# A fourth key block selected by bisection, thirteen steps earlier; one gate in the indexer; two passes on other engines

## The chip, the core and the metric

The kernel runs on one core of a Trainium2 chip. The metric is the device time of one execution in microseconds (us). The median of three runs of the kernel before is 1662.06 us (1661.48 to 1665.17).

The engines are named as the profile names them: PE (matrix products), PEld (the loads of PE's weights), DVE (vector), ACT (scalar functions), POOL (GpSimd) and SP (here it only issues DMAs). Each engine works through its own queue in order.

## The reference

One decoder layer on 1024 tokens of width 1024 in float32. An input projection feeds two attention branches of 8 heads each; the second one attends only to the 256 keys that an indexer scores highest for the query. The branches are gated, merged and projected, and a SwiGLU block follows.

```python
proj = x @ w_in[l]
(fq, fk, fv, f_logit, dq, dk, dv, iq, ik, iw, g_a, g_b) = _split_columns(proj)
...
rel = relu(einsum('bqhd,bkd->bqhk', iqb, ik))              # indexer
score = einsum('bqh,bqhk->bqk', iwb * IDX_SCALE, rel)
score = where(kpos <= qpos, score, NEG_INF)
_, idx = lax.top_k(score, topk)                             # topk = 256
...
merged = sigmoid(g_a) * (o_a @ w_branch_a[l]) + sigmoid(g_b) * (o_b @ w_branch_b[l])
x = layer_norm(ALPHA * x + merged @ w_out[l])
gate, up = split(x @ w_ffn_in[l], 2)
x = layer_norm(ALPHA * x + (silu(gate) * up) @ w_ffn_out[l])
```

## The kernel before

Every float32 product is made of three passes (`mm3`, L96): each operand is split into a rounded high part, which ACT writes, and the rest, a low part that DVE or POOL subtracts (`load_w`, L86, for the weights of the projections: high part on ACT, low part on POOL).

The program has these stages.

- **Indexer** (L242 to L285). Four pieces `c` of the indexer's query weights, two heads each. For each head and each block `i` of 128 queries from 2 to 7, PE makes the scores S (L270, L271), ACT applies relu into one of three tiles `r` (L273, L275), and DVE adds them into the score tile `SM[i]` (L277, L279). `SM[i]` has 128 rows of queries and 128(i+1) keys. Here the order on every engine, PE too, is set by the scheduler that builds the program.
- **Attention** (L540 to L602), 64 steps: eight units of a head pair, two heads, four groups G of two query blocks in the order 3, 0, 2, 1. PE's order is written out by hand: in step k the scores of step k+1 (`weigh`), the transposes and sums of step k (`average`), and between them single groups of three matmuls from a list of filler work: the projections of the next unit and the 16 gates, `NG` of them in each unit. The other engines' order is the scheduler's, which follows the order of the program text where two instructions are both ready. A step's path runs S on PE (L463, L466), maximum on DVE (L473), exp on ACT (L474), reciprocal on DVE (L480), scaling on POOL (L483), transposes on PE (L506), high part on ACT (L507), low part on DVE (L508), sums on PE (L515, L516).
- **Selection of 256 keys** for blocks 2 to 7, needed when the second branch begins at step 32. It is written into the program at step `KSEL` = 31, and the scheduler fills gaps of DVE and ACT with it from the end of the indexer on. Blocks 2, 3 and 4 go by `select_by_max` (L287): 32 times a DVE instruction that finds eight maxima (L290) and one that strikes them out (L291). Blocks 7, 6 and 5 go by `select_by_bisection` (L294): 32 rounds, each of which counts on ACT how many scores of each block are above a threshold (L310, one instruction a block) and then sets the next threshold with three small DVE instructions (L311, L320, L318). At its end DVE makes the masks in pieces of 512 keys (L348 to L361); L361 is the last pass, which turns 1 and 0 into 0 and a large negative number.
- **Branch products, output product, first layer norm** (L605 to L772), not touched.
- **SwiGLU** by a scheme of fewer products (L775 to L904). For each of 22 chunks, DVE makes four sums of weights (`ss`, L843 to L846), and `split` (L793) makes the parts: high on ACT, low on POOL (L795).
- **Output of SwiGLU** (L909 to L1014), not touched.

Of the kernel before, what the change touches and what calls it, by code (L numbers as in the profile page):

```python
# [8 lines left out]
F32 = mybir.dt.float32  # L9
# [11 lines left out]
KT = 8  # L21
# [10 lines left out]
LAG = 2  # L32
W = (1, 1, 1, 1)
PW = 512
BIS = ((7, 6, 5),)
IDX_SCALE = (8 ** -0.5) * (64 ** -0.5)

NMM, NT = 2, 2
AHEAD, LASTC, HURRY = 3, 8, 100
NG = (1, 1, 2, 2, 2, 2, 2, 4)  # L40
ORDER = (3, 0, 2, 1)
PHB, PLB = 3, 3
A1 = (1, 2, 2, 2)
VD, LEAD, KSEL = 4, 5, 31

C_FQ, C_FK, C_FV, C_DQ, C_DK, C_DV, C_IQ, C_GA, C_GB, C_MISC = 0, 4, 8, 12, 16, 20, 24, 28, 36, 44

# [2 lines left out]
def trunk_kernel(ctx: ExitStack, tc: tile.TileContext, xT, xn, wt, wbr, wout, wfi, wfo,  # L50
# [187 lines left out]
    sp.dma_start(ald.rearrange("h r t -> (h r) t"), f(arr[0:16]))  # L238
    sp.dma_start(alkd, f(arr[32:34]))


    for c in range(4):  # L242
        w = split_w(raw0, pool) if c == 0 else load_w(wt[C_IQ + c])
        iq = [idx.tile([128, 768], F32R, name="iq", tag="iq", bufs=4) for _ in range(2)]
        for q, (half, c0, n, d0) in enumerate(((0, 256, 256, 0), (1, 0, 512, 256))):
            ps = ps_mm()
            proj_half(ps[:, :n], w, half, c0=c0, n=n)
            for a in range(2):
                src = ps[a * 64:a * 64 + 64, :n]
                t = iq[a][:, d0:d0 + n]  # L250
                act.activation(t[0:64], src, AF.Copy)
                dve.tensor_tensor(t[64:128], src, f(t[0:64]), op=OP.subtract)
        for a in range(2):
            h = 2 * c + a
            for i in range(2, 8):
                n = 128 * (i + 1)
                nch = 1 if n <= 512 else 2
                m = n // nch
                if nch == 1 and i == 2:
                    S = [psA.tile([128, 512], F32, name="S", tag="O", bufs=1)]  # L260
                elif i == IDXT:
                    S = [psA.tile([128, 512], F32, name="S", tag="T", bufs=NT) for _ in range(2)]
                else:
                    S = [ps_s(nch)]
                lq = iq[a][:, (i - 2) * 128:(i - 1) * 128]
                r = idx.tile([128, L], F32, name="r", tag="r", bufs=3)
                rv = r[:, :n].rearrange("p (a b) -> p a b", a=nch)
                for x in range(nch):
                    o = S[x][:, :m] if len(S) == nch == 2 else (S[0][:, x, :m] if nch == 2 or i == 3 else S[0][:, :m])
                    te.matmul(o, lq, ik1[:, x * m:x * m + m], start=True, stop=False)  # L270
                    te.matmul(o, lq, ik2[:, x * m:x * m + m], start=False, stop=True)  # L271
                    if len(S) == nch:
                        act.activation(rv[:, x], o, AF.Relu, scale=wab[:, i - 2, h:h + 1])  # L273
                if len(S) < nch:
                    act.activation(rv, S[0][:, :, :m], AF.Relu, scale=wab[:, i - 2, h:h + 1])  # L275
                if h == 0:
                    dve.tensor_scalar(SM[i], r[:, :n], sgn[:, i - 2, h:h + 1], None, op0=OP.mult)  # L277
                else:
                    dve.scalar_tensor_tensor(SM[i], r[:, :n], sgn[:, i - 2, h:h + 1], SM[i],  # L279
                                             op0=OP.mult, op1=OP.add)  # L280
    for i in range(2, 8):
        dg = SM[i][:, i * 128:]
        pool.affine_select(dg, dg, pattern=[[-1, 128]], base=0, channel_multiplier=1,
# [10 lines left out]
    def select_by_bisection(blocks, tag):  # L294
# [50 lines left out]
        for x, i in enumerate(blocks):  # L345
# [4 lines left out]
            for c in range(0, 128 * (i + 1), 512):  # L350
# [7 lines left out]
                if c + m < 128 * (i + 1):  # L358
                    dve.tensor_tensor(ci, ci, cum[:, m - 1:m], op=OP.subtract)
                dve.scalar_tensor_tensor(Sc, Sc, ki, e, op0=OP.is_gt, op1=OP.add)  # L360
                dve.tensor_scalar(Sc, Sc, BIG, BIG, op0=OP.mult, op1=OP.subtract)  # L361


    at, _at = open_pool("at")

    def proj_steps(ps, w, half):

        hi, lo = w
        for k in range(KT):
            mm3(ps, [(hi[:, k * 128:k * 128 + 128], lo[:, k * 128:k * 128 + 128],  # L370
                      XH[half][:, k], XL[half][:, k])], k == 0, k == KT - 1)
            yield

    def gate(br, c):
        w = load_w(wt[(C_GA, C_GB)[br] + c])
        for h in range(2):
            ps = ps_mm()
            yield from proj_steps(ps, w, h)
            g = at.tile([128, 512], F32, name="g", tag="g", bufs=2)
            if (br, c) == (1, 7):  # L380
                with tc.high_priority(offset=HURRY):
                    act.activation(g, ps, AF.Tanh, scale=0.5)
            else:
                act.activation(g, ps, AF.Tanh, scale=0.5)
            sp.dma_start(gdr[br][c, :, h * 512:h * 512 + 512], g)

    def project(br, pr, made):
        qc, kc, vc = ((C_FQ, C_FK, C_FV), (C_DQ, C_DK, C_DV))[br]
# [144 lines left out]
            sp.dma_start(odr[br][hd // 2, r0:r0 + 64, G * 256:G * 256 + 256], o)  # L533
            yield

    gates = [gate(br, c) for br in range(2) for c in range(8)]
    units = [[] for _ in range(8)]
    late = []

# [37 lines left out]
    for k, (n, a, G) in enumerate(todo):  # L577
# [4 lines left out]
        slots = [back] * nb  # L582
        slots.insert(A1[G], ahead)
        slots.insert(0, ahead)
        if k == KSEL:
            for blocks in BIS:
                select_by_bisection(blocks, blocks[0])
            for i in range(2, 8):
                if not any(i in blocks for blocks in BIS):
                    select_by_max(i)  # L590
# [199 lines left out]
        ring.append(at_)  # L790
        return at_[0].tile([128, 2, 512], F32R, name="w", tag=at_[1], bufs=at_[2])

    def split(s, raw):  # L793
        act.activation(s[:, 0], raw, AF.Copy)  # L794
        pool.tensor_tensor(s[:, 1], raw, f(s[:, 0]), op=OP.subtract)  # L795

    def product(ps, w, x, first=True, last=True):
        mm3(ps, [(w[:, 0, k * 128:k * 128 + 128], w[:, 1, k * 128:k * 128 + 128], x[0][:, k], x[1][:, k])
# [35 lines left out]
    for c in range(FC):  # L834
# [12 lines left out]
        if new:  # L847
            split(a11, g1_)
            split(a12, g2_)
        split(s2, r2)  # L850
        split(s3, r3)
        split(s1, r1)
        split(s4, r4)
# [214 lines left out]
```

## Time and profile before

| | |
|---|---|
| median of three runs | 1662.06 us |
| the profiled execution | 1662.34 us |
| its span, first to last instruction | 1660.5 us |
| busy in the span: PE, DVE, ACT, POOL | 96%, 69%, 47%, 45% |

The span is what the profile covers; 1.8 us of the execution lie around it. A busy share is an average over stages with different limits. A matmul is drawn longer than the time for which it holds PE, so PE's idle time shows only part of what a wait costs; the number of matmuls in a stretch shows the rest.

### The profile page before, as it was taken

How to read it: one execution, taken by the hardware profiler on the slowest of the kernel's cores; microseconds unless marked ns; L12 is line 12 of the kernel's file. 1: busy time of each engine (PE TensorE's matmuls, PEld its weight loads, DVE VectorE, ACT ScalarE, POOL GpSimd, SP SyncE). 2: the span in 40 equal slices, each digit the busy share in tenths (PEclk: the TensorE clock that was granted, in tenths of full speed). 3: DMA queues.
4: the chain of work that ended last, by engine and by line, in shares of the span. 5: the costliest groups of instructions: out<-in, count | busy, mean ns of one | idle time of the engine just before them, and what ended most of it. 6: DMA issues, size and time to landing. Idle time of an engine off the chain costs nothing. (4 is left out here: it accounts for less than half of the span.)

```text
span 1660.5 us, 22523 instructions
## 1 busy us (share of the span) xinstructions
PE 1601.0 (96%) x7722; PEld 1309.5 (79%) x7722; DVE 1139.2 (69%) x1986; ACT 772.6 (47%) x1374; POOL 749.9 (45%) x748
## 2 busy tenths in 40 slices
PE   7899999999999999999899998999999999999997
PEld 5777887777788888888778877778888888878886
DVE  6889999988744444444585665666666666757686
ACT  6777887885444545455442024223222322354341
POOL 1122333332323333334452044766777676487673
PEclk9999999999999999999999998999999999999999
DMA  5112212121212121212776112554445444598652
GB/s 179 47 40 66 61 46 60 51 72 46 61 53 77 52 77 52 77 52 76 260 248 226 58 59 93 194 172 149 155 154 168 152 146 134 180 328 307 194 163 100
DMA packets 96379, 202.83 MB, mean 122 GB/s; under 512 B 10820, under 2 KB 37444, under 8 KB 96264
## 3 DMA queue, kind: packets, MB, share of 16 engines
q1 hardware_dynamic: 96264, 201.39, 37.4%
q8 instruction: 61, 1.00, 0.3%
q14 instruction: 54, 0.44, 0.1%
HBM read 139.40 MB, written 53.03 MB: 116 GB/s over the span
## 5 line engine op out<-in xcount | busy, mean ns | idle before, releaser
L99 PE MATMUL mm<-xh,whi 128*128 128x512 f32 (+1 forms) x720 | 296.9, 412 | 14.1 <-ACT whi L147 6.5
L101 PE MATMUL mm<-xl,whi 128*128 128x512 f32 (+1 forms) x720 | 282.1, 392 | 1.0 <-DVE xl L157 0.9
L100 PE MATMUL mm<-xh,wlo 128*128 128x512 f32 (+1 forms) x720 | 281.4, 391 | 0.5 <-DVE wlo L148 0.5
L483 POOL TENSOR_SCALAR p<-p,st 128x512 f32<-128x512 f32 (+1 forms) x192 | 113.8, 602 | 318.7 <-DVE st L480 266.0
L93 POOL TENSOR_TENSOR wlo<-wraw,whi 128x1024 fp32r<-128x1024 f32 x43 | 103.4, 2406 | 164.2 <-ACT whi L92 164.1
L101 PEld LDWEIGHTS mm<-xl,whi 128*128 128x128 f32 x720 | 136.2, 189 | 32.2 <-DVE xl L157 2.2
L99 PEld LDWEIGHTS mm<-xh,whi 128*128 128x128 f32 x720 | 137.3, 191 | 28.6 <-ACT whi L147 6.5
L795 POOL TENSOR_TENSOR w<-ss,w 128x512 fp32r<-128x512 f32 x88 | 121.9, 1404 | 73.4 <-ACT w L794 73.4
L100 PEld LDWEIGHTS mm<-xh,wlo 128*128 128x128 f32 x720 | 137.5, 191 | 13.0 <-DVE wlo L148 1.0
L508 DVE TENSOR_TENSOR pl<-T,ph 128x512 fp32r<-128x512 f32 (+1 forms) x160 | 100.6, 634 | 36.6 <-ACT ph L507 33.7
L100 PE MATMUL acc<-fs 128*128 128x512 f32 x308 | 120.1, 390 | 1.3 <-DVE fs L935 1.3
L101 PE MATMUL acc<-fs 128*128 128x512 f32 x308 | 119.9, 389 | 0.6 <-POOL fs L936 0.6
L99 PE MATMUL acc<-fs 128*128 128x512 f32 x308 | 119.8, 389 | 0.0
L507 ACT ACTIVATE ph<-T 128x512 fp32r<-128x512 f32 (+1 forms) x160 | 87.3, 552 | 40.7 <-PE T L506 38.2
L310 ACT ACTIVATE junk<-sm,nt 128x1024 bf16<-128x1024 f32 (+2 forms) x93 | 96.8, 1040 | 14.5 <-DVE nt L318 12.6
L506 PE MATMUL T<-identf,p 128*128 128x128 f32 x576 | 91.0, 274 | 5.0 <-POOL p L483 2.9
L936 POOL TENSOR_TENSOR fs<-fraw,fs 128x512 fp32r<-128x512 f32 x47 | 80.8, 1733 | 27.1 <-ACT fs L934 27.1
L506 PEld LDWEIGHTS T<-identf,p 128*128 128x128 f32 x576 | 71.6, 140 | 27.0 <-POOL p L483 4.6
L812 ACT ACTIVATE u<-u 128x512 f32<-128x512 f32 x22 | 13.9, 632 | 168.2 <-DVE u L811 168.2
L843 DVE TENSOR_TENSOR ss<-wup 128x512 f32<-128x512 f32 x22 | 34.4, 1565 | 83.4 <-POOL w L795 71.5
L516 PE MATMUL O<-pl,V 128*128 128x256 f32 x320 | 82.9, 282 | 1.8 <-DVE pl L508 1.8
L515 PE MATMUL O<-ph,V 128*128 128x256 f32 x320 | 83.9, 284 | 0.0
(285 smaller groups left out, 4259.3 us busy)
## 6 DMA issues: line engine op xcount, KB each, us to landing
wraw<-in_wt_dram SPq DMA_DIRECT2D x45, 512.0 KB
fraw<-abd SPq DMA_DIRECT2D x30, 512.0 KB
wraw<-in_wfi_dram SPq DMA_DIRECT2D x25, 512.0 KB
wup<-in_wfi_dram SPq DMA_DIRECT2D x22, 512.0 KB
wb<-in_wfo_dram SPq DMA_DIRECT2D x44, 256.0 KB
abd<-wb SPq DMA_DIRECT2D x88, 128.0 KB
abd<-h SPq DMA_DIRECT2D x44, 256.0 KB
abd<-u SPq DMA_DIRECT2D x33, 256.0 KB
```

What stands on the lines that cost most here:

```text
L93: pool.tensor_tensor(lo, raw, f(hi), op=OP.subtract)
L99: te.matmul(ps, ah, bh, start=(first and i == 0), stop=False)
L100: te.matmul(ps, al, bh, start=False, stop=False)
L101: te.matmul(ps, ah, bl, start=False, stop=(last and i == n - 1))
L310: act.activation(j[:, :128 * (i + 1)], SM[i], AF.Sign, bias=bias(x), accum_out=s[:, x:x + 1])
L483: pool.tensor_scalar(pc, pc, st[:, 3:4], 1.0, op0=OP.mult, op1=OP.mult)
L506: te.transpose(T[:, s * 128:s * 128 + 128], P[qq][:, j * 128:j * 128 + 128], identf)
L507: act.activation(ph[:, c:], T[:, c:], AF.Copy)
L508: dve.tensor_tensor(pl[:, c:], T[:, c:], f(ph[:, c:]), op=OP.subtract)
L515: te.matmul(O, V[:, j, :], ph[:, r0:r0 + 256], start=(j == 0), stop=False)
L516: te.matmul(O, V[:, j, :], pl[:, r0:r0 + 256], start=False, stop=(last and jj == 1))
L795: pool.tensor_tensor(s[:, 1], raw, f(s[:, 0]), op=OP.subtract)
```

## The change

Five edits. (1) `BIS` takes block 4 into the bisection, so each round counts four blocks and `select_by_max` is left with blocks 2 and 3. (2) The bisection is written into the program at step `KBIS` = 18 instead of 31. (3) The masks' last pass (L361 before) is a POOL instruction. (4) Gate 0 leaves the attention's filler and is computed in the indexer, one half in piece 0 and one in piece 1; `NG` falls from 2 to 1 in unit 2, and the gates of units 0 to 2 move up by one, so that unit 2 (steps 16 to 23) has one gate fewer. (5) In the first chunk of SwiGLU the low part of `s2` is subtracted on DVE instead of POOL.

```diff
-BIS = ((7, 6, 5),)
+BIS = ((7, 6, 5, 4),)
-NG = (1, 1, 2, 2, 2, 2, 2, 4)
+NG = (1, 1, 1, 2, 2, 2, 2, 4)
-VD, LEAD, KSEL = 4, 5, 31
+VD, LEAD, KBIS, KSEL = 4, 5, 18, 31
...
+    def half_gate(br, c, w, h, tile):
+        ps = ps_mm()
+        yield from proj_steps(ps, w, h)
+        g = tile()
...
+            act.activation(g, ps, AF.Tanh, scale=0.5)
+        sp.dma_start(gdr[br][c, :, h * 512:h * 512 + 512], g)
...
+        if c == 0:
+            wg = load_w(wt[C_GA])
+        first = half_gate(0, 0, wg, c, lambda: idx.tile([128, L], F32, name="r", tag="r", bufs=3)[:, :512]) \
+            if c < 2 else iter(())
...
+                if a or i > 4:
+                    next(first, None)
+        for _ in first:
+            pass
...
-                dve.tensor_scalar(Sc, Sc, BIG, BIG, op0=OP.mult, op1=OP.subtract)
+                pool.tensor_scalar(Sc, Sc, BIG, BIG, op0=OP.mult, op1=OP.subtract)
...
-    gates = [gate(br, c) for br in range(2) for c in range(8)]
+    gates = [gate(br, c) for br in range(2) for c in range(8)][1:]
...
-        if k == KSEL:
+        if k == KBIS:
             for blocks in BIS:
                 select_by_bisection(blocks, blocks[0])
+        if k == KSEL:
             for i in range(2, 8):
...
-    def split(s, raw):
+    def split(s, raw, eng=pool):
         act.activation(s[:, 0], raw, AF.Copy)
-        pool.tensor_tensor(s[:, 1], raw, f(s[:, 0]), op=OP.subtract)
+        eng.tensor_tensor(s[:, 1], raw, f(s[:, 0]), op=OP.subtract)
...
-        split(s2, r2)
+        split(s2, r2, pool if c else dve)
```

How the queues move is shown at three places. The line numbers of the changed kernel are 11 to 27 higher for the same code; rows of before stand first.

PE in the indexer, from the scores of the first head's block 3 on (`S` are scores, `mm_568` is the projection of piece 1, `mm_502` the gate's first half):

```order
L270 MATMUL S_474<-ik1_275,iq_408 128x512
L271 MATMUL S_474<-ik2_276,iq_408 128x512
L99 MATMUL mm_568<-xh0_78,whi_562 128x256
L100 MATMUL mm_568<-xh0_78,wlo_563 128x256
L101 MATMUL mm_568<-xl0_79,whi_562 128x256
L270 MATMUL S_514<-ik1_275,iq_409 128x384
L271 MATMUL S_514<-ik2_276,iq_409 128x384
L99 MATMUL mm_568<-xh0_78,whi_562 128x256
L100 MATMUL mm_568<-xh0_78,wlo_563 128x256
L270 MATMUL S_480<-ik1_275,iq_408 128x320
```

In the changed kernel, at the same place:

```order
L293 MATMUL S_480<-ik1_275,iq_408 128x512
L294 MATMUL S_480<-ik2_276,iq_408 128x512
L99 MATMUL mm_502<-xh0_78,whi_470 128x512
L100 MATMUL mm_502<-xh0_78,wlo_471 128x512
L101 MATMUL mm_502<-xl0_79,whi_470 128x512
L99 MATMUL mm_502<-xh0_78,whi_470 128x512
L100 MATMUL mm_502<-xh0_78,wlo_471 128x512
L293 MATMUL S_486<-ik1_275,iq_408 128x320
L294 MATMUL S_486<-ik2_276,iq_408 128x320
```

The gate's matmuls take the places between scores that the next piece's projection had, and that projection moves behind them.

ACT in the attention, from the 20th to the 21st step (`junk` is a count of the bisection, `p` an exp, `ph` a high part, `Q1` and `K1` parts of a projection, `o` the end of a step):

```order
L310 ACTIVATE junk_4700,s7_4458<-sm7_196,nt7_4453 128x1024
L310 ACTIVATE junk_4702,s7_4458<-sm6_195,nt7_4453 128x896
L474 ACTIVATE p_3265,st_3266<-S_3259,st_3266 128x1024
L530 ACTIVATE o_3289<-O_3222 64x256
L310 ACTIVATE junk_4704,s7_4458<-sm5_194,nt7_4453 128x768
L507 ACTIVATE ph_3311<-T_3310 128x512
L474 ACTIVATE p_3303,st_3304<-S_3299,st_3304 128x128
L399 ACTIVATE Q1_3160<-mm_3252 64x512
```

In the changed kernel, in the 21st step:

```order
L337 ACTIVATE junk_3449,s7_3154<-sm7_196,nt7_3149 128x1024
L518 ACTIVATE ph_3823<-T_3822 128x512
L337 ACTIVATE junk_3451,s7_3154<-sm6_195,nt7_3149 128x896
L421 ACTIVATE K1_3080<-mm_3742 64x512
L337 ACTIVATE junk_3453,s7_3154<-sm5_194,nt7_3149 128x768
L421 ACTIVATE K1_3084<-mm_3742 64x512
L337 ACTIVATE junk_3455,s7_3154<-sm4_193,nt7_3149 128x640
L485 ACTIVATE p_3843,st_3844<-S_3839,st_3844 128x256
L518 ACTIVATE ph_3850<-T_3849 128x512
```

A round now has four counts, and in steps 19 to 23 almost every second instruction of ACT's queue is one. Counted in the whole queue, steps 12 to 23 hold 45 counts before and 64 now.

DVE at the end of the 25th step, where the masks are made (`junk` and `e`, `cum` are mask passes, `pl` the low part that the step's last sums need):

```order
L473 TENSOR_REDUCE st_3776<-S_3771 128x1
L357 SCALAR_TENSOR_TENSOR e_4780<-cum_4781,s7_4458,e_4780 128x512
L508 TENSOR_TENSOR pl_3786<-T_3784,ph_3785 128x512
L480 RECIPROCAL st_3776<-st_3776 128x1
L359 TENSOR_TENSOR s7_4458<-s7_4458,cum_4781 128x1
L360 SCALAR_TENSOR_TENSOR sm7_196<-sm7_196,k7_4460,e_4780 128x512
L349 TENSOR_SCALAR s7_4458<-s7_4458 128x1
L348 TENSOR_SCALAR junk_4813,s7_4458<-sm5_194,k7_4460 128x768
L361 TENSOR_SCALAR sm7_196<-sm7_196 128x512
L508 TENSOR_TENSOR pl_3805<-T_3803,ph_3804 128x384
```

In the changed kernel, up to the same low part:

```order
L376 TENSOR_SCALAR s7_3154<-s7_3154 128x1
L375 TENSOR_SCALAR junk_3558,s7_3154<-sm6_195,k7_3156 128x896
L383 SCALAR_TENSOR_TENSOR cum_3544<-e_3543 128x512
L376 TENSOR_SCALAR s7_3154<-s7_3154 128x1
L375 TENSOR_SCALAR junk_3576,s7_3154<-sm5_194,k7_3156 128x768
L384 SCALAR_TENSOR_TENSOR e_3543<-cum_3544,s7_3154,e_3543 128x512
L376 TENSOR_SCALAR s7_3154<-s7_3154 128x1
L375 TENSOR_SCALAR junk_3594,s7_3154<-sm4_193,k7_3156 128x640
L386 TENSOR_TENSOR s7_3154<-s7_3154,cum_3544 128x1
L387 SCALAR_TENSOR_TENSOR sm7_196<-sm7_196,k7_3156,e_3543 128x512
L376 TENSOR_SCALAR s7_3154<-s7_3154 128x1
L519 TENSOR_TENSOR pl_4270<-T_4268,ph_4269 128x384
```

Before, five mask instructions stand between that low part and the reciprocal ahead of it; now there are fifteen, of which the last eleven are shown.

## Rows read from the trace of the kernel before

**Rows 1.** The page: PE's line of section 1 and PE's granted clock in 40 slices
```profile
PE 1601.0 (96%) x7722; PEld 1309.5 (79%) x7722; DVE 1139.2 (69%) x1986; ACT 772.6 (47%) x1374; POOL 749.9 (45%) x748
...
PEclk9999999999999999999999998999999999999999
```

**Rows 2.** Windows: stretch, its length, busy us (instructions) of each engine, granted clock, DMA
```profile
core 0: us, PE busy (x) PEld busy (x) DVE busy (x) ACT busy (x) POOL busy (x), PEclk, DMA share, GB/s
32.00:76.00 44.00, 36.75 (x188) 29.89 (x187) 35.57 (x47) 33.65 (x47) 6.06 (x3) 1.00 0.14 34
...
162.00:253.00 91.00, 89.55 (x498) 72.87 (x496) 88.76 (x223) 73.38 (x155) 30.23 (x53) 1.00 0.20 55
253.00:379.00 126.00, 120.73 (x660) 97.56 (x658) 112.12 (x254) 105.28 (x212) 41.70 (x68) 1.00 0.22 62
379.00:410.00 31.00, 27.22 (x136) 21.93 (x135) 27.50 (x67) 14.65 (x31) 7.25 (x12) 0.89 0.10 31
410.00:441.00 31.00, 28.73 (x150) 22.89 (x149) 28.00 (x45) 13.29 (x27) 12.39 (x16) 1.00 0.20 67
441.00:503.00 62.00, 62.00 (x344) 52.00 (x343) 28.62 (x64) 30.57 (x63) 21.66 (x34) 1.00 0.22 59
1016.00:1028.00 12.00, 8.31 (x25) 6.30 (x24) 8.44 (x9) 6.17 (x12) 11.07 (x9) 0.72 0.22 68
```

**Rows 3.** Windows of L310 alone: ACT's busy us (rows, two a count)
```profile
253.00:379.00 126.00, 50.29 (x90) 1.00 0.22 62
```

**Rows 4.** Waits of PE's weight loads, 30 to 110 us: total us, times, longest
```profile
PEld S L270 <- ACT r L275: 9.7, 18, 3.0
```

**Rows 5.** Waits of PE's weight loads, 110 to 441 us
```profile
PEld S L463 <- ACT p L474: 7.4, 10, 1.3
...
PEld T L506 <- DVE pl L508: 4.1, 5, 1.9
```

**Rows 6.** Timeline of PE at 48 us: start, us, what
```profile
48.27 0.39 PE L99 MATMUL mm<-xh,whi 128*128 128x512 f32 x1
48.49 0.40 PE L100 MATMUL mm<-xh,wlo 128*128 128x512 f32 x1
```

**Rows 7.** Groups by shape, DVE, 100 to 440 us: busy us, mean ns | idle before
```profile
L290 DVE MAX8 m<-sm 128x8 f32<-128x640 f32 x32 | 26.1, 817 | 0.1
L291 DVE MATCH_REPLACE8 sm<-m,sm 128x640 f32<-128x640 f32 x32 | 25.8, 808 | 0.0
```

**Rows 8.** Groups by shape, ACT, 100 to 440 us: the bisection's counts
```profile
L310 ACT ACTIVATE junk<-sm,nt 128x1024 bf16<-128x1024 f32 x31 | 35.6, 1147 | 13.8 <-DVE nt L318 12.6 <-DVE mp L329 0.9
L310 ACT ACTIVATE junk<-sm,nt 128x896 bf16<-128x896 f32 x31 | 32.2, 1040 | 0.4
...
L310 ACT ACTIVATE junk<-sm,nt 128x768 bf16<-128x768 f32 x31 | 29.0, 934 | 0.4
...
L310 ACT ACTIVATION_READ_ACCUMULATOR junk<-sm,nt 128x1 f32 x93 | 17.9, 192 | 0.0
```

**Rows 9.** Groups by shape, DVE, 100 to 440 us: passes of the masks
```profile
L356 DVE TENSOR_TENSOR_SCAN cum<-e 128x512 f32<-128x512 bf16 x4 | 6.6, 1645 | 0.0
L360 DVE SCALAR_TENSOR_TENSOR sm<-sm,k,e 128x512 f32<-128x512 f32 x4 | 3.0, 748 | 0.0
...
L348 DVE TENSOR_SCALAR_CACHE_REDUCE junk<-sm,k 128x768 bf16<-128x768 f32 x1 | 1.0, 1001 | 0.0
```

**Rows 10.** Timelines of DVE and POOL at 430 us
```profile
429.77 2.64 DVE L361 TENSOR_SCALAR sm<-sm 128x256 f32<-128x256 f32 x1
...
429.54 2.45 POOL L93 TENSOR_TENSOR wlo<-wraw,whi 128x1024 fp32r<-128x1024 f32 x1
```

**Rows 11.** Timelines of PE, DVE and POOL in SwiGLU's first chunk
```profile
1022.43 0.80 PE L100 MATMUL pb<-t2h,w 128*128 128x512 f32 x1 [3.69 <-POOL w L795]
...
1017.04 1.79 DVE L846 TENSOR_TENSOR ss<-wraw,ss 128x512 f32<-128x512 f32 x1
...
1019.36 0.68 DVE L843 TENSOR_TENSOR ss<-wup 128x512 f32<-128x512 f32 x1
...
1021.12 1.26 POOL L795 TENSOR_TENSOR w<-ss,w 128x512 fp32r<-128x512 f32 x1
```

More of the change, by code (lines that the diff above doesn't have):

```diff
@@ L239, in trunk_kernel, with proj_steps @@
     sp.dma_start(alkd, f(arr[32:34]))
+    def proj_steps(ps, w, half):
+        hi, lo = w
+        for k in range(KT):
+            mm3(ps, [(hi[:, k * 128:k * 128 + 128], lo[:, k * 128:k * 128 + 128],
+                  XH[half][:, k], XL[half][:, k])], k == 0, k == KT - 1)
+            yield
+    def half_gate(br, c, w, h, tile):
+        ps = ps_mm()
+        yield from proj_steps(ps, w, h)
+        g = tile()
+        if (br, c) == (1, 7):
+            with tc.high_priority(offset=HURRY):
+                act.activation(g, ps, AF.Tanh, scale=0.5)
+        else:
+            act.activation(g, ps, AF.Tanh, scale=0.5)
+        sp.dma_start(gdr[br][c, :, h * 512:h * 512 + 512], g)
     for c in range(4):
@@ L360, in select_by_bisection @@
                 dve.scalar_tensor_tensor(Sc, Sc, ki, e, op0=OP.is_gt, op1=OP.add)
-                dve.tensor_scalar(Sc, Sc, BIG, BIG, op0=OP.mult, op1=OP.subtract)
+                pool.tensor_scalar(Sc, Sc, BIG, BIG, op0=OP.mult, op1=OP.subtract)
     at, _at = open_pool("at")
[L366 to L372, printed above, removed]
     def gate(br, c):
@@ L376, in gate @@
         for h in range(2):
[L377 to L385, printed above, removed]
+            yield from half_gate(br, c, w, h, lambda: at.tile([128, 512], F32, name="g", tag="g", bufs=2))
     def project(br, pr, made):
```

## The prediction

> **What bounds the kernel now.** I read the page first. PE is busy for 1601 of 1660.5 us [rows 1], so whatever the change does counts only where PE waits or where PE has less to do. The slices are too coarse to show where that is, so I cut the span into stretches. From 441 to 503 us, when the selection is over, PE is busy in every microsecond and does 344 matmuls in 62.00 us, 0.180 us each [rows 2]. That is the pace of the attention with no other engine in its way, and I measure the earlier stretches by it; their mix of matmuls is nearly the same.
>
> - 162 to 253 us: 498 matmuls would take 89.6 us at that pace, the stretch took 91.
> - 253 to 379 us: 660 would take 118.8, it took 126. DVE is busy for 112.12 and ACT for 105.28 of it [rows 2].
> - 379 to 410 us: 136 would take 24.5, it took 31, at a granted clock of 0.89, so part of it ran at 1.2 instead of 2.4 GHz. DVE is busy for 27.50.
> - 410 to 441 us: 150 would take 27.0, it took 31, with DVE busy for 28.00 [rows 2].
>
> So the selection costs PE some 19 us between 162 and 441 us, and DVE is the busiest of the other engines in all four stretches. The waits agree: PE's weight loads stand for an exp on ACT (7.4 us in ten waits) and for low parts on DVE (4.1 us in five) [rows 5]. In the indexer PE is idle for 7.25 us between 32 and 76 us [rows 2], mostly because a score tile has not been read yet by the relu on ACT (9.7 us in 18 waits of the loads, pieces 2 and 3 included) [rows 4]. In SwiGLU's first chunk there is one wait of 3.69 us for a low part on POOL [rows 11].
>
> **The gate in the indexer.** It takes 48 matmuls of 512 columns out of steps 16 to 23 and puts them into pieces 0 and 1. Two such matmuls start 0.22 to 0.23 us apart [rows 6], so this is 10.9 us of PE on both sides. PE's idle time there is 7.25 us, and the order puts the gate's matmuls between the scores where PE waits. If they fill it, the indexer gets longer by 10.9 - 7.25 = 3.6 us. If they fill none of it, by 10.9; if they also fill what the drawn-out ends of matmuls hide, by nothing. I take **+3.5 us**, near the row of PE's idle time, and keep 0 to +8. What comes along costs nothing: one high part on ACT and one low part on POOL, both with idle time there (33.65 and 6.06 busy of 44) [rows 2], two Tanh on ACT, and two stores on SP. Behind these stores SP's queue has weights that are needed only by the first projections, some 30 us later. A store holds one of the three `r` tiles until it lands; the next piece's projection, which needs no `r`, covers that. Without that cover a store's time would be lost to the relu twice.
>
> **Block 4 by bisection.** DVE loses 32 maxima of 817 ns and 32 strikes of 808 ns [rows 7], 52 us in all, most of it between 253 and 379 us. ACT gets 32 more counts. The counts of 1024, 896 and 768 keys take 1147, 1040 and 934 ns [rows 8], 106 ns less for each 128 keys, so I estimate 828 ns for 640 keys, and 192 ns to read the sum. What matters is where they fall.
>
> - Up to step 11 (162 to 253 us) blocks 2 and 3 are still searched by maxima, so DVE stays as full as it was (88.76 of 91), and each round puts one more count on ACT, which has 73.38 of 91 [rows 2]. Ten rounds add some 9 us there. Nothing is relieved. I take **+1.0 us**, between 0 and +3.
> - Steps 12 to 23 (253 to 379 us). The 45 counts of before are busy for 50.29 us [rows 3], 1.118 us each. With 640 keys in the mix the mean falls by 0.053 us (the mean of 1147, 1040, 934 and 828 is 987, of the first three 1040). The order now holds 64 counts in these steps: 64 x 1.065 = 68.2 us, 17.9 more. The gate takes about 2.2 us away (a high part and two Tanh). ACT's load is 105.3 + 17.9 - 2.2 = 121 us. PE's need falls to 118.8 less seven eighths of 10.9, which is 109. DVE's falls from 112 to about 60. So ACT takes DVE's place as the engine that sets the pace, with 121 us of work for a stretch that took 126. Part of the busy time is the tail of an instruction beside the next one, and ACT's queue has a count or a step's instruction ready nearly always. Against that, a step's exp and high parts now wait for one count more each time. I take 123.5 us, **-2.5 us**. The lower end is PE's need and the 4 us for waits that no edit touches, 115 (-11). The upper end is ACT at 93% of the time, 130 (+4).
>
> **Thirteen steps sooner, and the masks.** The order finishes the bisection in the 23rd step, as before: the earlier place in the program makes up for the longer rounds, it does not bring the masks forward. But the masks now stand ahead of the steps in the program, and the scheduler puts them into DVE's queue in larger blocks. Their work grows by block 4: two count passes (1001 ns at 768 keys, so near 0.9 each), a scan of 1645 ns and a smaller one, and four compare passes of 750 ns or less [rows 9], about 7 us. The last pass, now on POOL, gives back some 4.9 us, 2.64 of it from a single instruction of 256 keys that ran beside a low part of POOL [rows 10]. DVE's load in 379 to 441 us stays near 57 of 62 us. In the 25th step, fifteen mask instructions stand between a reciprocal and the low part that the step's last sums need: 0.9 to 1.3 us for each of four counts, 1.6 for the scan, three passes of 0.5 to 0.75 and seven small ones, about 7 us. PE has about 3.5 us of other work until then (three groups of filler and eight sums), so I expect one wait of about **4 us** there and, as after the waits of before, a few microseconds at 1.2 GHz. Before, this stretch lost 6.5 us in several waits; PE has one eighth of the gate less in it. I set the two stretches to **-1.0 us**, between -4 and +4. POOL's last passes go behind its scaling of the probabilities; with 19.6 of 62 us busy there [rows 2] they cost nothing, and without that slack up to eight times 0.6 us.
>
> **The low part on DVE.** POOL makes the first chunk's `s2` low part as its third and ends it at 1022.4 us, and PE starts then. On DVE it goes behind the sum that is followed by the instruction at 1019.36, so it would end at 1020.0 at 0.68 us, or at 1021.1 at the 1.79 us that a subtraction of the same shape took beside POOL [rows 11]. PE starts 1.3 to 2.4 us sooner, and a shorter wait can save time at the lower clock, which was 0.72 on average here [rows 2]. The next product needs a low part that POOL makes now at about the same time as before, so some of it is lost again. **-1.5 us**, between -4 and +0.5.
>
> The row of 1.79 us fits a rule of the Trainium skill, "SBUF — State Buffer", section "Who interferes with whom": a DVE instruction with two inputs in SBUF and a GpSimd instruction that reads SBUF cannot use the port that they share at the same time, and the second waits. This speaks against the fifth edit and for the third. By the rule alone the low part would end at 1021.1 and the term would be about -1; without it -2.5.
>
> **Sum.** +3.5 + 1.0 - 2.5 - 1.0 - 1.5 = -0.5 us on the profiled execution of 1662.34 us. The median lies 0.28 us lower, so I forecast **1661.6 us**, no change that can be measured. A measurement of this kernel tells about 0.2%, 3.3 us, from no change.
>
> **Rivals.**
>
> *Faster: DVE was the limit, and ACT holds.* For it speaks that DVE is the busiest in all the slow stretches. If ACT's counts fit between the step's own instructions, 253 to 379 us shrink to 115 (-11), and with the other terms the sum is -9: **1653 us**. Against it: ACT's load of 121 us is above PE's 109.
>
> *Slower: ACT's queue becomes the wait.* Place: steps 18 to 23, where every second instruction is a count. Each exp and each high part stands behind a count of about 1 us, and PE, whose score tiles and transpose tiles come free only through them, stands too. Price: with ACT at 93%, the stretch takes 130 us (+4), and the wait at the masks brings +2 in place of -1; with the other terms as taken 3.5 + 1.0 + 4 + 2 - 1.5 = +9: **1671 us**. It decides against the change as soon as ACT can't be kept busy for 97% of the stretch. Against it: before, ACT was idle only 12.6 us for the bisection's own chain [rows 8], and DVE, which answers it, is free now.
>
> *The masks don't come sooner and the gate is only moved.* This is the forecast itself, 1661.6 us: time taken from steps 16 to 23 on PE is given to ACT, and the gate is paid in the indexer.
>
> **How the numbers follow.** Forecast (within 0.2%): 0.38. Faster rival: 0.33, since a wait less for DVE may give more than the loads show. Slower rival: 0.29. The range reaches into both: with the stretch at 115 the sum is -9, 1653, and the fastest tenth beyond that is left out; with the slower rival's sum it is 1671, and what is above that is left out. I give 1653 to 1671. The likeliest case's own range is 1659 to 1665.
>
> **What would show it.** In the changed kernel: the indexer's last score 3 to 4 us later; the end of the 11th step about 4 us later; between there and the 23rd step's end about 123 us, with ACT busy for over 95% and DVE for under 60%; one wait of PE for a low part on DVE of about 4 us in the 25th step; the wait in SwiGLU's first chunk 1 to 2 us shorter. The forecast is wrong if steps 12 to 23 take under 119 or over 128 us, or if the indexer takes as long as before.

## The result, and the profile after

The changed kernel takes 1672.28 us, median of six runs (1669.45 to 1676.23); the kernel before, run beside it, 1661.50 us. The ratio is 1.0069, with a 95% interval of 1.0058 to 1.0080: **slower by 0.7%**, 1.3 us outside of the forecast's range (1653 to 1671), with the sign of the slower rival. The profiled execution took 1670.48 us, which lies inside the range, with a span of 1668.7 us. So the profiles explain 8.2 of the 10.8 us between the medians; the other 2.6 lie between executions, and no profile shows them.

The page of the changed kernel, its span and its busy times [rows 1]:

```profile
span 1668.7 us, 22516 instructions
...
PE 1602.4 (96%) x7722; PEld 1312.3 (79%) x7722; DVE 1095.3 (66%) x1899; ACT 797.5 (48%) x1438; POOL 761.9 (46%) x755
```

PE's busy time has hardly changed, DVE lost 44 us and ACT got 25: the change did to the engines' loads what it says. To see where the time went I compare marks of the work: the end of the sum `o` that closes an attention step (L531 before, L542 now), and in SwiGLU the start of the same matmul, counted from PE's last one. The table shows what each stretch of work added to the lead or the lag of a kernel against the kernel before, each in its profiled execution; the first line is the length of the stretch before. "SwiGLU 0" goes from 1009 to 1066 us of the kernel before; the last stretch is the rest. Steps are counted from 1 here; `KBIS`, `KSEL` and the steps named with them count from 0.

| kernel | to end of step 1 | steps 2-11 | 12-18 | 19-23 | 24-28 | 29-64 | to SwiGLU | SwiGLU 0 | rest | to the last matmul |
|---|---|---|---|---|---|---|---|---|---|---|
| before (us) | 161.9 | 91.1 | 71.6 | 54.3 | 62.2 | 358.3 | 209.4 | 57.5 | 585.3 | |
| changed | +10.3 | +2.0 | -6.4 | +4.3 | +0.8 | -0.4 | +0.3 | -3.4 | +0.9 | +8.5 |
| gate_back | -4.0 | +2.2 | -4.5 | +5.5 | +1.5 | -0.7 | -1.5 | -3.4 | +2.4 | -2.5 |
| gate_only | +9.2 | +0.8 | -6.3 | -5.8 | -2.8 | +2.0 | -1.6 | -0.1 | -0.7 | -5.2 |
| own_tile | +4.7 | +2.0 | -6.4 | +5.5 | +3.0 | -0.4 | -0.9 | -3.4 | +1.2 | +5.4 |
| split_back | +10.3 | +2.0 | -6.4 | +4.3 | +0.7 | -0.4 | +0.6 | -0.0 | -1.8 | +9.3 |
| gate_own | +4.4 | +0.8 | -6.2 | -6.1 | -2.0 | +1.6 | -1.1 | -0.1 | -0.1 | -8.7 |
| bis_back | +10.2 | +0.8 | -6.3 | +2.8 | -6.6 | -0.2 | -0.2 | -3.4 | +1.9 | -1.0 |
| kbis31 | +11.1 | +2.0 | -6.2 | -5.7 | -5.6 | +7.7 | +1.4 | -3.4 | +1.5 | +2.7 |
| gate_own_split | +4.6 | +0.7 | -6.2 | -6.1 | -2.2 | +1.6 | -1.3 | -3.4 | +2.1 | -10.1 |
| mask_back | +9.1 | +2.0 | -6.3 | +4.4 | +1.4 | -1.7 | +0.3 | -3.4 | +1.6 | +7.4 |
| best_mask | +4.5 | +0.7 | -6.2 | -6.1 | -0.9 | -0.3 | +0.4 | -3.4 | +1.6 | -9.7 |
| best_k24 | +3.8 | +0.7 | -6.2 | -6.1 | +2.4 | -0.8 | +0.7 | -3.3 | +2.5 | -6.3 |

So the changed kernel has lost everything when the first step ends, and the rest of it wins 1.8 us back. The last score of the indexer ends at 120.83 us, where it was 109.68: 11.2 us, the gate's 10.9 us of PE in full. The windows of the changed kernel, for the stretches of [rows 2], show it as well (the stretch, its length, busy us and instructions of each engine, granted clock, DMA):

```profile
core 0: us, PE busy (x) PEld busy (x) DVE busy (x) ACT busy (x) POOL busy (x), PEclk, DMA share, GB/s
32.00:76.00 44.00, 36.16 (x165) 28.93 (x164) 30.02 (x41) 30.19 (x41) 5.05 (x2) 0.96 0.15 38
...
172.20:265.40 93.20, 90.03 (x499) 73.02 (x498) 88.97 (x222) 82.20 (x174) 29.83 (x52) 1.00 0.19 54
...
265.40:389.10 123.70, 115.50 (x629) 92.61 (x629) 65.51 (x159) 118.02 (x249) 36.45 (x65) 0.99 0.20 51
389.10:452.10 63.00, 52.38 (x264) 41.76 (x263) 58.00 (x119) 28.15 (x58) 36.12 (x38) 0.95 0.19 56
```

In the first row PE is idle for 7.84 us, where it was 7.25 before: most of the gate is in this stretch (its second half up to the 20th of 24 matmuls), and none of the idle time is gone. In the third row ACT is busy for 118 of 123.7 us and DVE for 65.5, as forecast.

**The indexer.** PE's timeline (start, us, what; in brackets the idle time before it and what ended it), then ACT's:

```profile
49.49 0.40 PE L101 MATMUL mm<-xl,whi 128*128 128x512 f32 x1
...
55.76 0.28 PE L101 MATMUL mm<-xl,whi 128*128 128x256 f32 x1
58.57 0.50 PE L99 MATMUL mm<-xh,whi 128*128 128x512 f32 x1 [2.54 <-ACT r L257]
...
59.46 0.63 PE L99 MATMUL mm<-xh,whi 128*128 128x512 f32 x1
59.89 0.63 PE L100 MATMUL mm<-xh,wlo 128*128 128x512 f32 x1
```

```profile
56.77 1.26 ACT L296 ACTIVATE r<-S,wab 128x512 f32<-128x512 f32 x2
57.92 0.60 ACT L257 ACTIVATE r<-mm 128x512 f32<-128x512 f32 x1
```

The first row is the last matmul of the gate's first half, done at 49.9 us. Its tanh (L257) starts at 57.92 us, 8 us later: it wants one of the three tiles `r`, and these go round between the relus on ACT and the sums on DVE. Until then the half gate holds one of the two accumulators `mm`. The 256 columns of piece 1's projection fill the other one by 56.0 us, and the 512 columns that must follow have none. So PE stands for 2.54 us, and the piece's scores, which stand behind that projection in PE's order, start at 65.75 us. Before, the 512 columns were made between the scores of piece 0, from 43.12 to 55.8 us (two of their matmuls are in [rows 6]), and the scores of piece 1 start at 55.60 us.

**Steps 19 to 23.** ACT's timeline at 338 us (`junk` is a count, `p` an exp, `ph` a high part) and PE's:

```profile
338.64 0.69 ACT L485 ACTIVATE p<-S,st 128x512 f32<-128x512 f32 x1
...
339.32 1.14 ACT L337 ACTIVATE junk<-sm,nt 128x1024 bf16<-128x1024 f32 x1
...
340.45 0.47 ACT L518 ACTIVATE ph<-T 128x384 fp32r<-128x384 f32 x1
```

```profile
340.98 0.38 PE L526 MATMUL O<-ph,V 128*128 128x256 f32 x1 [2.54 <-ACT ph L518]
```

PE stops at 338.44 us and waits for a high part that stands behind an exp and a count of 1024 keys. The same happens at 362.2 us (1.29 us). In all PE waits 7.2 us in these steps: 3.8 for high parts on ACT, 2.4 for POOL's scaling and 1.0 for low parts on DVE.

**Step 25.** The wait that the prediction named is there, and matmuls of 512 columns behind it start 0.43 us apart and not 0.23:

```profile
414.09 0.48 PE L527 MATMUL O<-pl,V 128*128 128x256 f32 x1 [4.51 <-DVE pl L519]
414.80 0.63 PE L99 MATMUL mm<-xh,whi 128*128 128x512 f32 x1
```

**SwiGLU.** The first chunk gains 3.4 us, and a chunk further on loses more. In the first chunk PE waits twice in place of the 3.69 us of before [rows 11], for the low part on DVE and, at the next product, for one on POOL:

```profile
1031.07 0.50 PE L100 MATMUL pb<-t2h,w 128*128 128x512 f32 x1 [1.35 <-DVE w L807]
...
1035.39 0.50 PE L100 MATMUL pb<-t3h,w 128*128 128x512 f32 x1 [1.26 <-POOL w L807]
```

The rest of the gain goes along with the clock. The granted clock of 18 us from the same matmul on was 0.81 and is 1.00 now; the windows of before and of the changed kernel:

```profile
1014.00:1032.00 18.00, 14.31 (x51) 11.09 (x50) 11.32 (x13) 6.98 (x13) 15.07 (x13) 0.81 0.29 91
```

```profile
1024.60:1042.60 18.00, 15.39 (x65) 11.88 (x65) 14.48 (x15) 7.49 (x14) 14.61 (x12) 1.00 0.27 92
```

PE, DVE and POOL at 1080 us:

```profile
1086.79 0.77 PE L99 MATMUL pb<-t3h,w 128*128 128x512 f32 x1 [4.22 <-DVE u L875]
```

```profile
1080.94 1.77 DVE L857 TENSOR_TENSOR ss<-wraw,wup 128x512 f32<-128x512 f32 x1 [4.32 <-POOL w L807]
```

```profile
1071.46 1.29 POOL L807 TENSOR_TENSOR w<-ss,w 128x512 fp32r<-128x512 f32 x1
1076.40 0.82 POOL L894 TENSOR_TENSOR wb<-wb 128x256 f32<-128x256 f32 x1 [3.65 <-DMA wb<-in_wfo_dram]
...
1079.61 2.54 POOL L807 TENSOR_TENSOR w<-ss,w 128x512 fp32r<-128x512 f32 x2
```

The scheduler has put four subtractions of output weights (`wb`) ahead of the low parts (`w`). They wait until 1076.40 us for a DMA; a sum of DVE (L857) waits for the low part behind them, and the sum `u` that PE needs stands behind that one on DVE.

### The profile page after: what moved, and what is told of

Same layout as the page of the kernel before. It is cut to its first block, busy times and chain, and to the rows that moved or that the text cites. A ratio compares the mean times of both kernels' runs of the same rounds, so it can differ in the third digit from the quotient of the medians.

```text
span 1668.7 us, 22516 instructions
## 1 busy us (share of the span) xinstructions
PE 1602.4 (96%) x7722; PEld 1312.3 (79%) x7722; DVE 1095.3 (66%) x1899; ACT 797.5 (48%) x1438; POOL 761.9 (46%) x755
## 4 chain that ended last, share of the span: by engine, by line
PE 71%; DVE 11%; ACT 6%; DMA 4%; POOL 4%; issue 4%; SPq 0%; DVEq 0%; POOLq 0%; ACTq 0%
PE pb L99 7%; PE pb L100 7%; PE pb L101 7%; PE mm L99 7%; PE mm L101 7%; PE mm L100 6%; PE acc L100 3%; PE acc L101 3%; PE acc L99 3%; PE ob L101 3%; PE ob L100 3%; PE ob L99 3%; PE T L517 3%; ACT junk L337 2%; PE S L477 2%
## 5 line engine op out<-in xcount | busy, mean ns | idle before, releaser
L337 ACT ACTIVATE junk<-sm,nt 128x1024 bf16<-128x1024 f32 (+1 forms) x124 | 122.3, 987 | 5.1 <-DVE nt L345 4.1
```

The source lines that it names most:

```text
L337: act.activation(j[:, :128 * (i + 1)], SM[i], AF.Sign, bias=bias(x), accum_out=s[:, x:x + 1])
```

## The experiments

Ratios are against the kernel before, run on the same chip.

**gate_back: the gate back in unit 2.** The changed kernel without edit 4.

```diff
-NG = (1, 1, 1, 2, 2, 2, 2, 4)
+NG = (1, 1, 2, 2, 2, 2, 2, 4)
...
-        first = half_gate(0, 0, wg, c, ...)
...
-    gates = [gate(br, c) for br in range(2) for c in range(8)][1:]
+    gates = [gate(br, c) for br in range(2) for c in range(8)]
```

> The changed kernel with edit 4 undone: gate 0 is filler of unit 2 again, the other four edits stay. The changed kernel ends its first attention step 10.3 us later than the kernel before (172.2 against 161.9 us). Theory A, the gate found no idle time of PE in the indexer and only pushed back the next piece's projection: the first step ends at 162 us again (-10); steps 12 to 23, which take 123.7 us in the changed kernel, get back seven eighths of the gate (9.5 us of PE) but ACT has 121 us of work there and hides most of it: 125 to 128 us (+1 to +4). Total -6 to -9 against the changed kernel's profiled span of 1668.7, so 1660 to 1663. Rival B, PE sets the pace in steps 12 to 23 of the changed kernel: these steps get longer by 9 us, and the total moves by under 2 us.

1661.25 us, ratio 1.0001 (0.9992 to 1.0010): the other four edits together change nothing. The indexer's last score ends at 110.02 us, 0.3 us later than before, so the gate costs 10.8 us there. Steps 12 to 23 take 126.9 us against 123.7:

```profile
251.20:378.10 126.90, 122.43 (x659) 98.73 (x657) 64.05 (x159) 123.18 (x257) 41.48 (x68) 0.99 0.22 62
```

Theory A: ACT is busy for 123.18 of 126.90 us and hides most of the gate. The first step ends at 157.9 us, 4 us sooner than was expected, and the span is 1657.7. DVE has half its load and the stretch is not shorter than before (125.9), but ACT's load has grown from 105.28 to 123.18 us, so this run alone does not tell whether DVE held the stretch before; the next one does.

**gate_only: edit 4 alone on the kernel before.** The changed kernel with the other four edits undone:

```diff
-BIS = ((7, 6, 5, 4),)
+BIS = ((7, 6, 5),)
...
-VD, LEAD, KBIS, KSEL = 4, 5, 18, 31
+VD, LEAD, KBIS, KSEL = 4, 5, 31, 31
...
-                pool.tensor_scalar(Sc, Sc, BIG, BIG, op0=OP.mult, op1=OP.subtract)
+                dve.tensor_scalar(Sc, Sc, BIG, BIG, op0=OP.mult, op1=OP.subtract)
...
-        split(s2, r2, pool if c else dve)
+        split(s2, r2)
```

> The kernel before with edit 4 alone (gate 0 in the indexer; three blocks by bisection, written at step 31, masks on DVE, the low part on POOL). Theory A: the first step's end moves from 161.9 to 172 us; steps 12 to 23 were held by DVE (112 us busy of 126) and shrink by no more than 3 us: total +7 to +10, 1669 to 1672. Rival B, PE's filler held these steps: they shrink by 8 or more, total +2 or less.

1658.60 us, ratio 0.9987 (0.9976 to 0.9999), slightly faster. It pays 9.2 us up to the first step, and steps 12 to 23 shrink by 12.1 us:

```profile
263.00:376.80 113.80, 111.46 (x622) 90.27 (x621) 107.27 (x242) 95.42 (x195) 38.98 (x66) 1.00 0.22 60
```

This is rival B, against theory A. PE's filler held these steps of the kernel before; with 38 matmuls fewer (622 for 660, some 8.5 us at the 0.22 to 0.23 us of [rows 6]) they take 113.8 us, and DVE is busy for 107.27 of them, where it was 112.12 of 126. So DVE was not their limit. The same edit saves 12.1 us here and 3.2 beside the other edits (126.9 to 123.7); kbis31, further on, shows which of them takes the difference.

**own_tile: the gate's tanh into a tile of its own.** The changed kernel with

```diff
-        first = half_gate(0, 0, wg, c, lambda: idx.tile([128, L], F32, name="r", tag="r", bufs=3)[:, :512]) \
+        first = half_gate(0, 0, wg, c, lambda: idx.tile([128, 512], F32, name="gg", tag="gg", bufs=1)) \
```

> The changed kernel, with the gate's tanh in the indexer written into a tile of its own instead of one of the three tiles r. In the changed kernel PE waits 2.54 us for this tanh at 56.0 us (the accumulator that the next projection needs is free only then) and runs 3.4 us at half the clock behind it. Theory A (displacement): the tanh comes at most 1 to 2 us sooner, the scores of the last piece end 0 to 2 us sooner, total -2 to 0. Rival C (the cost of the gate is this wait for tile and accumulator): -4 to -7, the first step ends at 166 to 168 us.

1666.63 us, ratio 1.0034 (1.0023 to 1.0046), so 0.35% better than the changed kernel. The last score ends 5.6 us sooner. The tanh now runs at 52.38 us, not at 57.92, and the wait of 2.54 us is gone:

```profile
52.38 0.60 ACT L257 ACTIVATE gg<-mm 128x512 f32<-128x512 f32 x1
```

Rival C: half of the gate's price in the indexer was the tile. The other half, 5.6 us at the last score and 4.7 at the first step, is left. The window from 32 to 76 us shows what the tile had hidden:

```profile
32.00:76.00 44.00, 39.77 (x192) 33.04 (x190) 32.89 (x45) 33.63 (x45) 6.09 (x3) 0.96 0.17 46
```

PE is idle for 4.23 us, where it was 7.25 before and 7.84 in the changed kernel: with the tile out of the way the gate does fill some of the idle time. The scheduler also orders PE's matmuls a little differently here, so the 5.6 us are those of the tile and of that order together. Of them 3.1 us are left at the last matmul; steps 19 to 28 take 3.4 us more than in the changed kernel.

**split_back: the low part of `s2` on POOL again.** The changed kernel with

```diff
-        split(s2, r2, pool if c else dve)
+        split(s2, r2)
```

> The changed kernel with edit 5 undone: the first chunk's s2 low part is made on POOL again. In the changed kernel SwiGLU's start is 3.4 us shorter than before, but at 1082 us PE waits 4.2 us for a sum of DVE that stood behind POOL, and the offset to the kernel before rises by 5.1 us there. Theory D: the edit moved the scheduler's order on POOL (four subtractions of output weights in a row, waiting for a DMA, ahead of low parts): with the edit undone the wait of PE at 1082 us is 1.3 us as before, and PE's wait of 3.7 us at the first chunk is back; end of span 2 to 3 us later than in the changed kernel (the part of the offset that it won back). Rival E: the wait at 1082 us comes from the DMA landing late and has nothing to do with the edit: it stays, and the end of span is 3.4 us later plus nothing won back.

1673.50 us, ratio 1.0070 (1.0056 to 1.0084): no difference to the changed kernel. The 3.4 us at the first chunk are gone, and so is the wait of 4.2 us at the later one (PE's longest wait from 1040 to 1110 us is 0.8). PE's order is the same in both; only POOL's, DVE's and ACT's differ. That is theory D, though the edit's net gain is 0.8 us in the profiles where 2 to 3 were expected.

**gate_own: the kernel before, with the gate in the indexer and the tile of its own.** The edits of gate_only and own_tile together.

> The kernel before with edit 4 alone, and the gate's tanh in the indexer written into a tile of its own. Two things were seen one by one: the gate alone pays 10.1 us in the indexer and gets 19 us back in steps 12 to 24 (of which 6 are lost again up to step 64), end of span -5.2; the own tile took 5.6 us off the indexer of the changed kernel. Theory C (half of the gate's price in the indexer is the wait for the tile and the accumulator): the last score ends 4.5 to 5 us later than before, end of span -9 to -11, median 1651 to 1655. Rival: a sooner start of the attention meets the selection's chain at the same time, the 5.6 us are eaten by waits in the steps: 1657 to 1660.

1653.52 us, ratio 0.9951 (0.9939 to 0.9963): -8.7 us in the profiles, just short of what was expected. The last score ends 6.4 us later than before, where 4.5 to 5 were expected: the tile gives 3.7 us there, and not 5.6. At the last matmul 3.5 us of it are left.

**bis_back: block 4 by maxima again.** The changed kernel with

```diff
-BIS = ((7, 6, 5, 4),)
+BIS = ((7, 6, 5),)
```

> The changed kernel with edit 1 undone: block 4 is searched by maxima on DVE again (written at step 31), the bisection has three blocks (written at step 18). In the changed kernel ACT is busy 118 of the 123.7 us of steps 12 to 23 and DVE 65.5. Theory F (with four blocks counted, ACT sets the pace of these steps, so the gate's removal there saves little): without block 4 they take 113 to 116 us as with the gate edit alone (113.8), the end of span comes 5 to 9 us sooner than in the changed kernel (1660 to 1664). Rival G (the earlier place in the program, not the fourth block, costs the time): they stay at 121 to 125 us.

1660.54 us, ratio 0.9985 (0.9976 to 0.9995). The span ends 9.8 us sooner than in the changed kernel, a little more than theory F has, but steps 12 to 23 take 122.4 us, and that is rival G: with three blocks the early place costs the time too. DVE, with block 4 to search again, is busy for 113.45 us of them, so this run alone does not part the place from DVE's load; kbis31 does. Where bis_back wins is in steps 24 to 28 (-6.6), since its bisection ends at 380.9 us, in step 23.

**kbis31: the bisection of four blocks written at step 31.** The changed kernel with

```diff
-VD, LEAD, KBIS, KSEL = 4, 5, 18, 31
+VD, LEAD, KBIS, KSEL = 4, 5, 31, 31
```

> The changed kernel with edit 2 undone: the bisection of four blocks is written at step 31 instead of 18. Theory F: ACT's work in steps 12 to 23 is nearly the same, so they stay at 120 to 125 us, and the end of span moves by under 3 us either way. Rival G (the earlier place costs the time, because a count stands before an exp): they shrink by 5 us or more, and the masks come later: steps 24 to 33 get longer by 2 to 4.

1665.68 us, ratio 1.0015 (1.0004 to 1.0026). Rival G again: steps 12 to 23 shrink by 9.9 us to 113.9. The masks come later, so steps 24 to 28 shrink by 6.4 us too and steps 29 to 64 get 8.1 us longer; steps 24 to 33 together take 119.3 us for 117.5. The windows of steps 12 to 18, 19 to 23 and 24 to 33, for the count's line alone, of the changed kernel and of this one (ACT's busy us; two rows a count):

```profile
265.40:330.50 65.10, 33.16 (x61) 1.00 0.22 57
330.50:389.10 58.60, 35.88 (x68) 0.97 0.17 43
389.10:506.60 117.50, 4.30 (x8) 0.97 0.20 58
```

```profile
266.20:331.50 65.30, 33.20 (x61) 1.00 0.22 58
331.50:380.10 48.60, 24.84 (x47) 1.00 0.22 61
380.10:499.40 119.30, 15.48 (x30) 0.97 0.18 53
```

The same window of gate_only for steps 19 to 23, with three blocks written at step 31, and all engines of kbis31 in steps 12 to 23:

```profile
328.30:376.80 48.50, 15.43 (x28) 1.00 0.23 60
```

```profile
266.20:380.10 113.90, 112.03 (x629) 91.58 (x629) 62.80 (x151) 108.90 (x228) 39.03 (x67) 1.00 0.22 59
```

Up to step 18 the changed kernel and kbis31 do the same in the same time. From there the place in the program decides: in steps 19 to 23 the changed kernel makes 11.0 us more of counts and takes 10.0 us longer, with PE waiting 7.2 us where it waits 0.9 in kbis31. A count that goes ahead of a step's own instruction costs nearly its full time. One that fills a gap costs nothing: kbis31 makes 9.4 us more of counts in these steps than gate_only, in the same time (48.6 and 48.5 us). Nor does ACT's busy share decide it: ACT is busy for 108.90 of 113.90 us here and for 118.02 of 123.70 in the changed kernel, over 95% in both. All that it buys is that the bisection ends at 395.5 us, in step 24, and not at 407.1, in step 26.

**gate_own_split: the gate with its own tile, and `s2` on DVE.** gate_own with edit 5.

> The kernel before with the gate in the indexer (its tanh in a tile of its own) and the first chunk's s2 low part on DVE, nothing else. Theory D (the scheduler puts POOL's rows in SwiGLU in another order when one is missing, so that low parts stand behind subtractions that wait for a DMA): 3.4 us gained at the first chunk, and between 0 and 5 us lost at a later chunk in one wait of PE for a sum of DVE; end of span -2.5 to +1.5 against the same kernel with the low part on POOL. Rival: the loss in the changed kernel came from its later or earlier arrival there: no wait over 1.5 us after the first chunk, -3.4 in full.

1652.97 us, ratio 0.9945 (0.9932 to 0.9958), not to be told from gate_own. Theory D: the 3.4 us are there, and PE waits 4.4 us for the sum `u` at the later chunk, with the same order on POOL as in the changed kernel from 447 us on and an arrival some 20 us sooner. So the wait goes with the order and not with the arrival. The other profiles agree: the nine kernels with edit 5 all have one wait of 4.2 to 4.5 us there; the four without it have none over 2.1 us there, and all wait 3.69 us in the first chunk. **This version is faster than the kernel before by 0.55% (0.42 to 0.68).**

**mask_back: the masks' last pass on DVE.** The changed kernel with

```diff
-                pool.tensor_scalar(Sc, Sc, BIG, BIG, op0=OP.mult, op1=OP.subtract)
+                dve.tensor_scalar(Sc, Sc, BIG, BIG, op0=OP.mult, op1=OP.subtract)
```

> The changed kernel with edit 3 undone: the masks' last pass on DVE. In the changed kernel DVE is busy 58.0 and POOL 36.1 of the 63.0 us of steps 24 to 28. Theory H (DVE sets the pace there, so the pass on POOL pays): these steps get 1 to 5 us longer, end of span +1 to +4. Rival I (the pass on POOL stands before the scaling of probabilities, and takes DVE's port): they get 1 to 4 us shorter.

1671.85 us, ratio 1.0051 (1.0035 to 1.0067), an interval that overlaps that of the changed kernel. Steps 24 to 28 get 0.6 us longer and steps 29 to 64 1.3 shorter; the 1.2 us that it gains up to the first step lie ahead of any mask. Neither theory H nor rival I: the edit is worth nothing that can be measured.

**best_mask: gate_own_split with edit 3.**

> The kernel before with edits 3, 4 (tanh in a tile of its own) and 5: block 4 by maxima, the bisection written at step 31. Against the same without edit 3 (span 1649.8 us, median 1653.0). Theory H: the masks lie in steps 26 to 30 there and cost some 8 us of waits; the pass on POOL takes some 2 to 5 us of DVE off them: -1 to -3, median 1650 to 1652. Rival I: POOL's scaling, for which PE waits 5.3 us in two waits there, comes later: +1 to +3.

1652.78 us, ratio 0.9938 (0.9923 to 0.9952): the same as without the edit; again neither.

**best_k24: gate_own_split with its bisection of three blocks written at step 24.**

> The kernel before with edits 4 (tanh in a tile of its own) and 5, and its bisection of three blocks written at step 24 instead of 31. With 31, 15 of the 96 counts are made in steps 23 to 25 and the masks in 26 to 30. What was seen of the place: with 18, ten counts move into steps 19 to 23, which get 10 us longer, each count costing its own 1 us. Theory F' (a count that goes ahead of a step's instruction costs its time wherever ACT is full, and a mask that goes ahead costs DVE's): up to step 23 nothing changes (within 0.5 us); from 24 on the masks are done sooner, in larger blocks: between -2 and +3, median 1651 to 1656. Rival: the sooner masks save the 8 us of waits of steps 26 to 30 for good: -4 or more.

1654.93 us, ratio 0.9949 (0.9932 to 0.9966). Up to step 23 nothing changes; steps 24 to 28 are 4.6 us longer than in gate_own_split, and 2.4 us come back in steps 29 to 64. The median is 2.0 us above that of gate_own_split, inside theory F'; the profiled execution, the longest of its four, is 3.8 us above in span, where the theory ends at +3. Either way the sooner masks don't pay for what they push back.

## Why the prediction was wrong, point by point

- **The gate in the indexer: +3.5 us (0 to +8) was forecast; it is +10.3 at the end of the first step.** This is the step that failed, and it carries 6.8 of the 9 us by which the sum was off. The last score, forecast 3 to 4 us later, is 11.2 us later. The sentence that failed is "A store holds one of the three `r` tiles until it lands; the next piece's projection, which needs no `r`, covers that." I looked at who needs `r` after the tanh and not at the tanh itself. The projection needs no `r`, but it needs the accumulator that the tanh has to read out first, and the tanh does need an `r`. The tile was worth 5.6 us up to the first step (own_tile). With it out of the way the gate costs 3.8 to 4.7 us there in five kernels, near the 3.5 that were taken. The rest of the reasoning was loose too: [rows 2] show that PE is idle for 7.25 us, but most of the idle time stood before scores that wait for a relu, and the order has a score next there, so the first waits stayed as they were. The gate took the places of the next piece's projection. What it filled behind them, the new wait took away (7.84 us idle); with the tile of its own 4.23 us are left.
- **Steps 2 to 11: +1.0 (0 to +3); measured +2.0.** The six kernels with three blocks and the gate in the indexer have +0.7 or +0.8, so block 4's counts cost some 1.2 us there.
- **Steps 12 to 23: -2.5, 123.5 us, with ACT busy for over 95% and DVE under 60%; measured 123.7, 95.4% and 53%.** The number is right, and PE does wait for ACT in steps 19 to 23; the reason is right only in part. It is not ACT's load that sets the pace but the place of the counts: kbis31 has ACT as full and takes 113.9 us. What I did not see is how much the other side of the choice was worth. That "the earlier place in the program makes up for the longer rounds" is true (the last count ends in step 24, as it did before), but it takes 10 of the 12 us that the gate's removal brings by itself (gate_only). And DVE, the busiest engine in all those stretches, had not been the limit: 38 matmuls fewer on PE gave 12 us with DVE's load nearly the same (gate_only). Two terms of the working were off as well: the matmuls in the stretch fell by 31 (660 to 629, some 7 us), not by seven eighths of the gate, so PE's need is some 112 us and not 109; and 109 with 4 us of waits make 113 for the lower end, not 115.
- **Steps 24 to 28: -1.0 (-4 to +4); measured +0.8.** The wait in step 25 was forecast as 4 us and is 4.51, with the lower clock behind it.
- **SwiGLU: -1.5 (-4 to +0.5); measured -2.5, as -3.4 and +0.9.** The wait became 2.3 us shorter, the upper end of what was taken, and the clock did not fall in this stretch. That some of it is lost again came true twice: 1.26 us at the next product, as forecast, and in the wait two chunks on that POOL's order makes, which I did not read from the order. Over whole runs the edit is worth nothing (split_back).
- **The low part of `s2` on DVE** took 0.68 us, not 1.79. It started at 1030.34 us, 0.02 us ahead of an instruction of POOL:

```profile
1030.34 0.68 DVE L807 TENSOR_TENSOR w<-ss,w 128x512 fp32r<-128x512 f32 x1
```

```profile
1030.36 1.80 POOL L807 TENSOR_TENSOR w<-wup,w 128x512 fp32r<-128x512 f32 x1
```

  POOL's took 1.80 us, where its row at 1071.46 us, shown further up, has 1.29 for the same shape. The Trainium skill, "SBUF — State Buffer", section "Who interferes with whom", says that issue order decides who blocks. This pair agrees; I had applied only the half of the rule in which DVE comes second, though the kernel before has the other half too: DVE's row at 1019.36 us took 0.68 [rows 11], and POOL's, 0.02 us behind it, 1.77.
- **The rivals.** The measured time is near that of the slower rival (1671), but by the gate: the rival had steps 12 to 23 at 130 us, and they take 123.7. Its mechanism is there all the same, in the place that it named: steps 19 to 23 are 4.3 us longer than before and 10 us longer than in kbis31, and the 6.4 us that steps 12 to 18 win hide it. The faster rival, DVE as the limit, is refuted by gate_only.

What stays open: the 2.6 us by which the medians differ more than the profiled executions, and what in the edits makes the stretch up to the end of the first step 4 us shorter in gate_back. All of that lies behind the last score (47.9 us from there, for 52.2 before): PE waits 1.8 us there and not 3.3, the granted clock is 1.00 and not 0.97, and the sum that closes the step ends 0.9 us after its last matmul and not 2.2.

## What to carry to other kernels

When a piece of work moves into another stage, list what it borrows there, tile by tile and accumulator by accumulator, and ask for each who has to let go of it first; PE's idle time is room for it only where the order has it next at that moment. Work that fills gaps is cheap only while it ranks behind the path's own instructions: 9.4 us of counts in gaps took no time, and 11 us of counts written earlier in the program took 10. And two edits that relieve the same stretch must be tried one by one: the gate alone gave 12 us there, and beside a bisection written ahead of the steps it gave 3.

## What was not expected of the hardware

Whether DVE or POOL pays when both read at the same time went by which began first, even by 0.02 us: 0.68 (DVE) and 1.80 us (POOL) in the pair above. At 1071.46 us it is the other way round: POOL's row there has 1.29 us, and DVE's, 0.07 us behind it, has

```profile
1071.53 1.76 DVE L855 TENSOR_TENSOR ss<-wup 128x512 f32<-128x512 f32 x1 [4.00 <-POOL w L807]
```

Waits of PE of one length were not followed by one clock. The stall of 2.54 us in the indexer was followed by seven matmuls of 512 columns 0.43 us apart (from 59.46 to 62.45 us), the pace at 1.2 GHz, where 0.23 us is that at 2.4. A wait of 2.56 us in the same kernel, which ended at 46.95 us, was followed by matmuls 0.23 us apart. And own_tile, which does not have the stall of 2.54 us, has matmuls of 512 columns 0.43 us apart from 38.50 us on. So the slow matmuls can't be put down to that stall. With the longer waits of SwiGLU (3.69 us in four kernels, 4.2 to 4.5 in nine) the granted clock fell every time.
